# Hybrid block on one core: key layout with half the transposes, gate factors spread over the items, a fixed order at the start of the up-projection

## The chip, the cores and the metric

The kernel runs on one core of one Trainium2 chip. The metric is the time on the device in microseconds of one execution; the median of several runs counts. Before the change it is 2391.09 us, the median of three runs between 2388.72 and 2391.73. One more execution was taken with the profiler on, and all views of the trace are of that one.

## What is computed

One layer of a decoder block with 2048 tokens of width 1024, all in float32. Cut to what matters here:

```python
h = rmsnorm(x, attn_norm)
z = h @ w_in            # pool channels | q | k | v | gate_pool | gate_attn
a = pool_mixer(u_pool, w_pool, pool_scale)          # causal means, windows 2/4/8/16
q = partial_rope(rmsnorm(q, q_norm), positions) * scale
k = partial_rope(rmsnorm(k, k_norm), positions)     # 2 heads of 64 for 16 query heads
b = swa_sink_attention(q, k, v, sinks)              # window 128
x = x + (g_pool * a + g_attn * b) @ w_out
h = rmsnorm(x, ffn_norm)
up = causal_depthwise_conv(h @ w_up, conv_w, conv_b)   # 2 x 2816 wide
x = x + (silu(gate) * val) @ w_down
```

## The kernel before

The tokens are worked off in two chunks of 1024 (`c` = 0 and 1), channels in slabs of 128. Every float32 operand is split into a high and a low half in the type float32r: ScalarE (ACT) casts the high half, VectorE (DVE) subtracts it to get the low half, and a product is three matmuls, high x high, high x low, low x high. `parted` (L1066) does this for activations, `split` (L245) for ordinary weights, `halved` (L360) for the factors below.

**Keys.** For each block of 128 tokens `block_b` (L783) rotates two key heads of 64 and writes their halves into `kd`, each of them twice side by side, and `turn` (L794) transposes them on TensorE (PE): four 128 x 128 transposes, for two heads and two halves. Every transpose gives a tile with the same 64 key channels in the upper and in the lower 64 partitions. `kts[g]` holds for head g the high tile and the low tile over the chunk. In `scores` (L884) the stationary operand has the queries' high half in the upper 64 partitions and the low half in the lower 64, so that two matmuls per query head, one by each tile, give all four partial products. The last block's keys of chunk 0 go to DRAM (`carry`) for chunk 1.

**Fast products.** The gates, the output projection and the up-projection use a scheme of seven products in place of eight for blocks of 2 x 2 (Winograd's form of Strassen's). The weight side needs sums of blocks, called A11, A12, A22, S1 to S4; the activation side B11, B21, B22, T1 to T4. `Blocks` (L341) makes the weight side of one unit in four steps: `first` (A11, A12), `second` (A22 and two sums on DVE), then `third` (S3, S2) and `fourth` (two sums on DVE, then S1, S4); for the first two gate units the fourth comes before the third. Each step has a cast on ACT and a subtraction on DVE (L362 and L363 for a whole slab, L378 and L379 in the second step). The sums stand in L382, L383, L390 and L391. `store` (L353) writes finished factors of these units to DRAM (`kept`), where chunk 1 reads them again through `Kept`. `R` is the tag of the raw weights, with three buffers; a unit holds two of them until its steps are done.

**Attention items and fillers.** `mixer` (L1926) runs 32 items per chunk: four groups of four query heads, eight blocks of 128 tokens each. An item has the scores of one block, the probabilities of the item before and the values of the one before that; between them PE is filled with projections (`fillers`, L144). In the last group of chunk 0 the fillers are gate and pooling projections, and the items also make the factors of the first two gate units: unit 0 in items 1, 2 (two steps) and 3, unit 1 in items 5 and 7, each behind the item's softmax chain on DVE (`tc.issue_after(chain)`). `store` is called in items 1 to 4 just ahead of the step and writes out all that is made so far.

**Up-projection.** `up` (L1504) works off 22 units. A unit has the products `one` to `seven`: `one` A11 x B11, `two` A12 x B21, `three` S2 x T2, `four` S1 x T1, `five` S3 x T3, `six` S4 x B22, `seven` A22 x T4. `one`, `three`, `five` and `seven` add up in one PSUM bank `x`; between them the bank is read, by an ACT copy (`kept`, L1441) after `one` and `three` and by a DVE add (L1467) after `five`. `product` (L1248) issues the twelve matmuls of one product. The activation side is made at the start (the head): `right_t1` to `right_t4` and `right_b22`, each of a difference on DVE (T2: L1228, T3: L1235, T4: L1245) and a `parted`. The loop over the other units takes `seven` and `six` of one unit between the products of the next; `conv` (L1482) follows on ACT and DVE.

**Order.** No order is written out for the engines. A planner goes through the program, estimates durations and lays out each engine's stream: when an engine is free it takes the earliest instruction of the program that is ready by its estimate. `tc.issue_after(ins)` adds an edge: what the block issues on the engine of `ins` stands behind `ins` there. It is an order and no wait between engines. Each stream, and the queue of transfers that SP issues, is then worked off in order on the chip.

## Time and profile before

| | before |
|---|---|
| median of three runs | 2391.09 us (2388.72 to 2391.73) |
| profiled execution | 2387.73 us |
| its span, first to last instruction | 2386.0 us |
| mean granted clock of TensorE | 0.999 |
| transfers through HBM | 408.10 MB, mean 171 GB/s |

The span is what the page's shares refer to; the profiled execution's own time has 1.73 us around it. PE is a matmul, PEld the load of its stationary operand, SP the engine that issues most transfers. `L1252` is line 1252 of the kernel; where a helper such as `product` or `parted` issues an instruction, the line is the helper's, and the tile's name tells which part of the program it serves (`f`, `t`, `a`, `s` are PSUM banks; `U`, `M`, `Q`, `F`, `R` are tags of SBUF tiles). Rows of the timeline give the start, the length, the engine, line and operation with its tiles and shapes, how many neighbours are merged in the row, and in brackets the idle time of the engine before it with what ended it. Rows of the waits give the total idle time, how often, and the longest.

### The profile page before, as it was taken

What the parts mean: (1) busy time and instruction counts of PE and PEld (TensorE: products, weight loads), DVE (VectorE), ACT (ScalarE), POOL (GpSimd) and SP (SyncE); (2) the same over time, 40 slices, a digit from 0 to 9 for tenths busy, and PEclk for the clock granted to TensorE, in tenths of its full rate; (3) what the DMA queues carried; (4) which work ended last, traced back from release to release, by engine and by line L of the source; (5) the groups of instructions that cost most, each with busy time, mean ns of one, the idle gap of its engine ahead of it and who ended that gap; (6) DMA issues with size and microseconds to landing.
All of it is one profiled execution on the core that took longest, in us unless ns stands there. A gap on an engine that the chain in (4) does not pass through costs nothing.

```text
span 2386.0 us, 30215 instructions
## 1 busy us (share of the span) xinstructions
PE 2359.7 (99%) x11080; PEld 1960.6 (82%) x11080; DVE 1912.9 (80%) x2938; ACT 1177.0 (49%) x2148; POOL 190.8 (8%) x142
## 2 busy tenths in 40 slices
PE   9999999999999999999999999999999999999999
PEld 8888888888788888788888888888878888888887
DVE  8688888877977777899956867788798777779994
ACT  7555455464654555543622544454445545554441
POOL 1123121010000000000002232200000000000000
PEclk9999999999999999999999999999999999999999
DMA  9767778687222233644454776666733222228421
GB/s 343 246 199 239 224 213 292 222 336 259 79 93 90 88 107 108 215 164 157 141 194 143 230 217 194 199 205 231 239 125 103 80 80 80 80 74 288 141 71 53
DMA packets 165028, 408.10 MB, mean 171 GB/s; under 512 B 14096, under 2 KB 50448, under 8 KB 155152
## 3 DMA queue, kind: packets, MB, share of 16 engines
q1 hardware_dynamic: 151584, 373.48, 46.2%
q0 software_dynamic: 8256, 24.12, 4.2%
q10 hardware_dynamic: 5040, 8.58, 1.0%
q8 instruction: 87, 1.43, 0.2%
q14 instruction: 61, 0.50, 0.1%
HBM read 267.32 MB, written 138.81 MB: 170 GB/s over the span
## 4 chain that ended last, share of the span: by engine, by line
PE 52%; DVE 3%; DMA 1%; ACT 1%; issue 1%; POOL 0%; SPq 0%; DVEq 0%; ACTq 0%; POOLq 0%
PE f L1252 12%; PE f L266 8%; PE t L1252 7%; PE f L1907 4%; PE a L1907 4%; PE s L1907 4%; PE t L1907 4%; PE a L1252 3%; PE a L960 1%; PE a L266 1%; PE s L899 1%; PE t L932 0%; DMA U<-made_pg 0%; PE f L1296 0%; DVE U L1070 0%
## 5 line engine op out<-in xcount | busy, mean ns | idle before, releaser
L266 PE MATMUL f<-U,U 128*128 128x512 f32 (+1 forms) x2088 | 489.4, 388 | 4.6 <-DVE U L250 1.8
L1252 PE MATMUL f<-U,U 128*128 128x512 f32 x1872 | 445.2, 390 | 4.1 <-DVE U L1070 2.4
L266 PEld LDWEIGHTS f<-U,U 128*128 128x128 f32 x2088 | 380.2, 188 | 81.2 <-DVE U L250 3.3
L1252 PEld LDWEIGHTS f<-U,U 128*128 128x128 f32 x1872 | 350.8, 188 | 79.4 <-DVE U L1070 3.1
L1489 DVE SCALAR_TENSOR_TENSOR M<-F,vc,M 128x1024 f32<-128x1024 f32 x176 | 225.3, 1281 | 141.1 <-ACT M L1486 140.7
L1252 PE MATMUL t<-U,U 128*128 128x512 f32 x1332 | 314.3, 389 | 0.3 <-ACT Q L1441 0.3
L1252 PEld LDWEIGHTS t<-U,U 128*128 128x128 f32 x1332 | 249.7, 188 | 53.1 <-ACT Q L1441 0.9
L362 ACT CAST U<-R 128x1024 fp32r<-128x1024 f32 x147 | 153.8, 1053 | 86.6 <-DVE R L391 43.9
L1252 PE MATMUL a<-U,U 128*128 128x512 f32 x756 | 183.7, 390 | 0.7 <-ACT Q L1441 0.7
L363 DVE TENSOR_TENSOR U<-R,U 128x1024 fp32r<-128x1024 f32 x147 | 179.2, 1221 | 0.3 <-ACT U L362 0.3
L1252 PEld LDWEIGHTS a<-U,U 128*128 128x128 f32 x756 | 141.2, 188 | 30.2 <-ACT Q L1441 1.2
L1252 PE MATMUL f<-U,M 128*128 128x512 f32 x624 | 150.2, 389 | 0.3 <-DVE F L1467 0.3
L918 ACT ACTIVATE Q<-s,st,rq 128x128 f32<-128x128 f32 x256 | 114.0, 456 | 65.5 <-DVE st L915 62.1
L1252 PEld LDWEIGHTS f<-U,M 128*128 128x128 f32 x624 | 117.0, 188 | 25.0 <-DVE F L1467 0.7
L940 POOL TENSOR_SCALAR_AFFINE_SELECT M<-M 128x1024 fp32r<-128x1024 f32 x64 | 94.3, 1474 | 380.2 <-DVE st L920 206.8
L1475 ACT COPY F<-f 128x512 f32<-128x512 f32 x52 | 30.6, 588 | 185.1 <-PE f L1252 185.1
L1865 ACT CAST U<-U 128x1024 fp32r<-128x1024 f32 x76 | 79.0, 1050 | 84.5 <-PE s L1907 22.0
L1486 ACT ACTIVATE M<-F,vc 128x1024 f32<-128x1024 f32 x88 | 109.3, 1243 | 2.4 <-DVE F L1471 1.0
L1866 DVE TENSOR_TENSOR U<-U,U 128x1024 fp32r<-128x1024 f32 x76 | 91.9, 1218 | 2.6 <-ACT U L1865 2.4
L1865 ACT CAST F<-U 128x1024 fp32r<-128x1024 f32 x44 | 46.2, 1050 | 93.8 <-PE a L1907 62.5
L967 ACT COPY U<-a 128x512 f32<-128x512 f32 x64 | 37.5, 586 | 105.1 <-PE a L960 104.9
L1441 ACT COPY Q<-f 128x512 f32<-128x512 f32 x104 | 61.0, 586 | 56.2 <-PE f L1252 56.1
(319 smaller groups left out, 4086.0 us busy)
## 6 DMA issues: line engine op xcount, KB each, us to landing
R<-w_up SPq DMA_DIRECT2D x80, 512.0 KB, 3.7
actd<-M SPq DMA_DIRECT2D x44, 512.0 KB, 2.7
U<-w_down SPq DMA_DIRECT2D x88, 256.0 KB, 4.9
U<-actd SPq DMA_DIRECT2D x88, 256.0 KB, 5.0
qd<-U SPq DMA_DIRECT2D x64, 256.0 KB, 3.8
Q<-qd SPq DMA_DIRECT2D x64, 256.0 KB, 4.9
R<-w_out SPq DMA_DIRECT2D x30, 512.0 KB, 4.5
U<-kept_S SPq DMA_DIRECT2D x12, 1024.0 KB, 6.6
```

The lines of the kernel that those rows point to most:

```text
L266: nc.tensor.matmul(out, a, b, start=(i == 0), stop=(i == n - 1))
L362: A.copy(t[:, 0], raw)
L363: V.tensor_sub(t[:, 1], raw, t[:, 0].bitcast(F32))
L918: A.activation(pr[:, h, :], sc[:, h, 0:P], AF.Exp, bias=nm[:, h:h + 1], scale=it["rq"][:, h:h + 1], accum_out=rs[:, h:h + 1])
L940: G.affine_select(own.rearrange("p a h q -> p (a h) q"), pa.bitcast(F32).rearrange("p a h q -> p (a h) q"), pattern=[[0, 8], [1, P]], base ...
L1252: nc.tensor.matmul(bank, a[:, x, k, :], b[k // 2][:, y, k % 2, :], start=(first and i == 0), stop=(i == 11), skip_group_check=True)
L1441: Up.last = A.copy(t, bank).ins
L1486: A.activation(y, u[:, 2:], AF.Identity, bias=cw[:, 3, m:m + 1], scale=cw[:, 2, m:m + 1])
L1489: V.scalar_tensor_tensor(y, u[:, j:j + T], cw[:, j, m:m + 1], y, op0=ALU.mult, op1=ALU.add)
L1865: A.copy(hi, src)
L1866: V.tensor_sub(lo, src, hi.bitcast(F32))
L1907: nc.tensor.matmul(into[m], u[:, 0, c_], v[:, 1], start=(first and j == 0), stop=(k == n - 1 and j == 2), skip_group_check=True)
```

## The change

Three parts of the kernel are changed.

1. Keys: `kd` holds for each head the high half in columns 0 to 63 and the low half in columns 64 to 127, so two transposes per block do; a transposed tile has the high half above and the low half below. `kts[0]` gets it by one DVE copy, `kts[1]` with the two halves exchanged by two ACT copies of 64 partitions. The scores use `kts[0]` and `kts[1]` where they used the high and the low tile; the sum of the two matmuls is the same.
2. Gate factors: unit 0's steps go to items 1, 2 and 3, and one to item 4 ahead of that item's fillers, behind the last weight split's cast on ACT. `store` writes in items 2 to 5 only what was made at least one item before.
3. Head of the up-projection: from `u0.four` to the end of the unit 3 round every product stands behind the product before it on PE. The first T3 difference stands behind the second T2 difference, the second T3 difference behind the second T2 tile's low half. T4 and the first later step of unit 2 stand behind T3's last low half on DVE. `u1.five` moves ahead of `u0.seven`.

```diff
-        def store(self, f, dma=load):
+        def store(self, f, only=None, dma=load):
...
-                if names not in done:
+                if names not in done and (only is None or names in only):
...
-            kd = kds[n] = qp.tile([P, 2, 2, P], F32R, "Q")
-            for d in range(2):
-                A.copy(kd[:, :, 0, d * HD:(d + 1) * HD], kn)
-                V.tensor_sub(kd[:, :, 1, d * HD:(d + 1) * HD], kn,
-                             kd[:, :, 0, d * HD:(d + 1) * HD].bitcast(F32))
+            kd = kds[n] = qp.tile([P, 2, P], F32R, "Q")
+            A.copy(kd[:, :, 0:HD], kn)
+            V.tensor_sub(kd[:, :, HD:P], kn, kd[:, :, 0:HD].bitcast(F32))
...
-            pt = ps.tile([P, 2, 2, P], F32R, "t")
+            pt = ps.tile([P, 2, P], F32R, "t")
             for g in range(2):
-                for a in range(2):
-                    nc.tensor.transpose(pt[:, g, a, :], kd[:, g, a, :], identr)
-            for g in range(2):
-                V.tensor_copy(kts[g][:, :, c_], pt[:, g].bitcast(F32))
+                nc.tensor.transpose(pt[:, g], kd[:, g], identr)
+            V.tensor_copy(kts[0][:, :, c_], pt.bitcast(F32))
+            for i in range(2):
+                A.copy(kts[1][64 * i:64 * i + 64, :, c_],
+                       pt[64 - 64 * i:128 - 64 * i].bitcast(F32))
...
-    def right_t3(xg, b):
+    def right_t3(xg, b, after=()):
         for j in range(2):
             q12, q22 = half(xg[j], 1), half(xg[j + 2], 1)
-            V.tensor_sub(q12, q22, q12)
+            with tc.issue_after(after[j]) if after else nullcontext():
+                V.tensor_sub(q12, q22, q12)
             b.setdefault("T3", []).append(parted(q12))
...
+        ordered = False
+
         def mul(self, bank, x, y, first=False):
-            product(bank, self.w.w[x], self.b[y], first)
+            with tc.issue_after(product.last) if Up.ordered else nullcontext():
+                product(bank, self.w.w[x], self.b[y], first)
...
         t2s = right_t2(xg, b, pb)
+        Up.ordered = True
         u0.four()
         u0.w.fetch("A22")
-        right_t3(xg, b)
+        right_t3(xg, b, (right_t2.sub, right_t2.low))
+        third = parted.low
...
         u0.five()
-        right_t4(xg, b, t2s)
-        weights(2, 1)
+        with tc.issue_after(third):
+            right_t4(xg, b, t2s)
+            weights(2, 1)
         u0.six()
         yg = u0.conv(0, u0.ug)
+        u1.five()
         u0.seven()
...
-        u1.five()
         for f in range(2, FT + 1):
+            Up.ordered = f < 4
...
             for g in range(2):
-                load(carry[g, :, 0:2], kts[g][:, :, T - P:T].bitcast(F32))
+                for a in range(2):
+                    load(carry[g, :, a], kts[a][:, g, T - P:T].bitcast(F32))
...
+            if c == 0 and group == 3 and n == 4:
+                with tc.issue_after(split_weights.last[0]):
+                    units[0].w.step()
...
                     if n == 0:
+                        older = []
                         stream.fetch(stream.used + 2)
-                    for f, steps in enumerate(({1: 1, 2: 2, 3: 1, 4: 0}, {5: 1, 7: 1})):
+                    for f, steps in enumerate(({1: 1, 2: 1, 3: 1, 4: 0, 5: 0}, {5: 1, 7: 1})):
                         if n in steps:
+                            w = units[f].w
                             if f == 0:
-                                units[f].w.store(units[f].f)
+                                w.store(units[f].f, older)
+                                older = list(w.tiles)
                             with tc.issue_after(chain):
-                                units[f].w.step(steps[n])
+                                w.step(steps[n])
```

More of the change, by code (lines that the diff above doesn't have):

```diff
@@ L886, in scores @@
         b = c * NB + n
-        kt = it["kts"][g]
+        kt = [t[:, g] for t in it["kts"]]
         if n == 0 and q4 == 3:
@@ L898, in scores @@
                 if n > 0:
-                    nc.tensor.matmul(sc[:, h, :], st, kt[:, a, (n - 1) * P:(n + 1) * P], **fl)
+                    nc.tensor.matmul(sc[:, h, :], st, kt[a][:, (n - 1) * P:(n + 1) * P], **fl)
                 else:
-                    nc.tensor.matmul(sc[:, h, P:256], st, kt[:, a, 0:P], **fl)
+                    nc.tensor.matmul(sc[:, h, P:256], st, kt[a][:, 0:P], **fl)
             if n == 0 and b > 0:
@@ L1069, in parted @@
         A.copy(t[:, 0], src)
-        V.tensor_sub(t[:, 1], src, t[:, 0].bitcast(F32))
+        parted.low = V.tensor_sub(t[:, 1], src, t[:, 0].bitcast(F32)).ins
         return t
@@ L1138, in out_proj @@
                     elif n * KT + m == at + 5:
-                        made.store(f, G.dma_start)
+                        made.store(f, dma=G.dma_start)
                 if n == 0 and m == 4:
@@ L1227, in right_t2 @@
             t2s.append(mp.tile([P, 2, 512], F32, "M"))
-            V.tensor_sub(t2s[j], half(xg[j + 2], 1), half(xg[j], 0))
+            right_t2.sub = V.tensor_sub(t2s[j], half(xg[j + 2], 1), half(xg[j], 0)).ins
             b.setdefault("T2", []).append(parted(t2s[j]))
+            right_t2.low = parted.low
         return t2s
-    def right_t3(xg, b):
+    def right_t3(xg, b, after=()):
         for j in range(2):
             q12, q22 = half(xg[j], 1), half(xg[j + 2], 1)
-            V.tensor_sub(q12, q22, q12)
+            with tc.issue_after(after[j]) if after else nullcontext():
+                V.tensor_sub(q12, q22, q12)
             b.setdefault("T3", []).append(parted(q12))
@@ L1251, in product @@
             for x, y in ((0, 0), (0, 1), (1, 0)):
-                nc.tensor.matmul(bank, a[:, x, k, :], b[k // 2][:, y, k % 2, :],
-                                 start=(first and i == 0), stop=(i == 11),
-                                 skip_group_check=True)
+                product.last = nc.tensor.matmul(bank, a[:, x, k, :], b[k // 2][:, y, k % 2, :],
+                                                start=(first and i == 0), stop=(i == 11),
+                                                skip_group_check=True).ins
                 i += 1
```

## The prediction, made before the changed kernel was run

> **What bounds the kernel now.** I read the page's first part (busy time of each engine) first, then the waits of TensorE, then the busy time by stage, and only then the order of single instructions around the longest waits.
>
> ```profile
> span 2386.0 us, 30215 instructions
> PE 2359.7 (99%) x11080; PEld 1960.6 (82%) x11080; DVE 1912.9 (80%) x2938; ACT 1177.0 (49%) x2148; POOL 190.8 (8%) x142
> ...
> PE f L1252 <- DVE U L1070: 2.4, 2, 1.3
> ...
> PE f L1252 <- ACT Q L1441: 1.4, 2, 0.7
> ...
> 575.00:645.00 70.00, 68.28 (x309) 55.88 (x308) 59.53 (x63) 35.77 (x52) 1.04 (x1) 1.00 0.40 146
> 1220.00:1305.00 85.00, 85.00 (x494) 74.54 (x493) 50.34 (x174) 25.05 (x69) 16.43 (x10) 1.00 0.43 139
> 1750.00:1815.00 65.00, 62.72 (x276) 50.96 (x275) 60.23 (x67) 34.43 (x44) 1.01 (x1) 1.00 0.24 81
> ```
>
> TensorE (PE) is the bound: it is busy 2359.7 of 2386.0 us, so 26.3 us of idle time is all that better order can win; anything else has to come from fewer PE instructions. The two wait rows (total, times, longest) are products of the up-projection (L1252) that wait for split operands (L1070) or for a bank to be copied out (L1441); both lie in code that the diff touches. The window rows give the length of the stage, then busy PE, weight loads, DVE, ACT and POOL. The two heads of the up-projection (575 to 645 and 1750 to 1815) have PE idle 1.7 and 2.3 us with DVE busy 85% and 93%: DVE sets the pace there. In the second chunk's keys (1220 to 1305) PE is never idle, so each transpose removed there comes straight off the end.
>
> **Keys by half the transpositions.**
>
> ```profile
> 1263.57 0.46 PE L799 MATMUL t<-identr,Q 128*128 128x128 f32 x4
> 1263.86 0.94 PE L266 MATMUL a<-U,U 128*128 128x256 f32 x6
> ...
> L799 PE MATMUL t<-identr,Q 128*128 128x128 f32 x64 | 7.2, 241 | 0.0
> L801 DVE CAST U<-t x32: 406/414/425, 42.3 to 1301.3; 128x256 fp32r<-128x256 f32 x32
> L790 ACT CAST Q<-Q x32: 293/298/308, 34.4 to 1279.9; 128x128 fp32r<-128x128 f32 x32
> L791 DVE TENSOR_TENSOR Q<-Q,Q x32: 274/285/295, 35.5 to 1280.2; 128x128 fp32r<-128x128 f32 x32
> L708 ACT COPY F<-f x16: 351/373/377, 12.1 to 72.0; 128x256 f32<-128x256 f32 x16
> ```
>
> A block of keys takes four transposes now and two after; 16 blocks make 32 fewer. Starts tell the price, since neighbours overlap: four begin at 1263.57 and the next matmul at 1263.86, so 0.29 us for four, 0.072 each, and 32 x 0.072 = 2.3 us. Their busy time shared out (7.2/64 = 0.112) would make it 3.6 us. I take 2.5, near the starts, because the busy figure counts overlap with the neighbours. [...]
>
> DVE loses one L791 and one L801 per block, 0.285 + 0.414 = 0.70 us. ACT loses one L790 and gains two copies of 64 partitions x 256 from PSUM; the nearest row is L708 (128x256 from PSUM, 373 ns), so ACT has 2 x 0.373 - 0.298 = 0.45 us more per block. In the second chunk both are hidden, since PE has no idle time there. In the first chunk's keys both engines feed PE closely, so the effect is bounded by one block's relief, -0.7, and one block's added ACT time, +0.45; I take -0.2. The two extra carry transfers happen once and lie on SP ahead of loads of weights and queries; at some 0.33 us of issue each (the SP rows below) they cost nothing as long as those loads land early, and 0.7 us at most.
>
> **Gate factors, one step per item.**
>
> ```profile
> 352.41 1.20 PE L266 MATMUL f<-U,U 128*128 128x512 f32 x4 [1.78 <-ACT U L249]
> ...
> 354.43 0.74 PE L266 MATMUL f<-U,U 128*128 128x512 f32 x2 [0.51 <-DVE U L250]
> ...
> 350.08 0.68 DVE L391 TENSOR_TENSOR R<-R,R 128x512 f32<-128x512 f32 x1
> ...
> 350.80 1.04 ACT L362 CAST U<-R 128x1024 fp32r<-128x1024 f32 x1
> 351.75 0.61 ACT L249 CAST U<-R 128x512 fp32r<-128x512 f32 x1
> ```
>
> The number in brackets is the idle time before a group and what ended it. Here PE stops 1.78 us for the high half of a pooling weight (L249), then 0.51 us for the low half (L250). On ACT that cast stands right behind L362, the cast of the gate unit's fourth step, which could begin only when DVE had finished L391 at 350.76. This is item 2 of the last group, the one with two steps; with one step the fourth moves to item 3, and L249 no longer stands behind it. PE's matmuls start 0.23 us apart but are drawn 0.39 long, so a stop costs about 0.16 more than its bracket: 1.78 + 0.51 + 2 x 0.16 = 2.6 us. I take 2.3, leaving 0.3 for what is late next; the bounds are 2.6 and nothing (the stop moves to item 3 or 4). The third step moves to item 4 and is put behind the last split's cast on ACT, so it cannot stand in front of that one. Each store to DRAM goes an item later, which takes its wait for L363 or L379 off SP; the copies are read in the second chunk only. One raw half of the unit is held an item longer, so the next unit's second raw half loads later; that is used only at item 7 and stays hidden.
>
> **The up-projection's head.**
>
> ```profile
> 600.46 1.21 DVE L1228 TENSOR_TENSOR M<-U,U 128x1024 f32<-128x1024 f32 x1
> 601.60 2.35 DVE L1235 TENSOR_TENSOR U<-U,U 128x1024 f32<-128x1024 f32 x2
> 603.87 1.21 DVE L1070 TENSOR_TENSOR U<-M,U 128x1024 fp32r<-128x1024 f32 x1
> ...
> 602.35 1.75 PE L1252 MATMUL f<-U,U 128*128 128x512 f32 x7
> 605.14 1.42 PE L1252 MATMUL f<-U,U 128*128 128x512 f32 x5 [1.04 <-DVE U L1070]
> 607.23 2.14 PE L1252 MATMUL f<-U,U 128*128 128x512 f32 x8 [0.67 <-ACT Q L1441]
> ...
> 1769.44 1.52 PE L1252 MATMUL f<-U,U 128*128 128x512 f32 x6
> 1771.23 0.50 PE L1252 MATMUL f<-U,U 128*128 128x512 f32 x1 [0.26 <-ACT U L1069]
> 1773.07 1.43 PE L1252 MATMUL f<-U,U 128*128 128x512 f32 x5 [1.34 <-DVE U L1070]
> 1775.18 1.20 PE L1252 MATMUL f<-U,U 128*128 128x512 f32 x4 [0.68 <-ACT Q L1441]
> ```
>
> In the first chunk PE stops in the middle of u0's third product, until the low half of the second T2 tile (L1070 at 603.87) is there. Both T3 differences (L1235) stand before it. With the new order only the first of them does; the low half then runs at 602.8 and ends about 604.0, and PE wants it at 603.9: the stop of 1.04 shrinks to about 0.2. The next stop, 0.67, is u0's fifth product, which follows its third at once and has to wait until ACT has copied the shared bank out (L1441). In strict order u1's third product stands between them and covers that copy. So 1.04 + 0.67 + 2 x 0.16 = 2.0 us go and 0.2 comes back. In the second chunk the same three stops make 0.26 + 1.34 + 0.68 + 3 x 0.16 = 2.8 us.
>
> What is late next: a unit's seventh product writes on the bank that the DVE add behind its fifth (L1467) must have read. Strict order puts u1's seventh right behind u0's, so one product stands between u1's fifth and seventh.
>
> ```profile
> 618.28 2.88 PE L1252 MATMUL f<-U,U 128*128 128x512 f32 x12
> 621.00 2.88 PE L1252 MATMUL t<-U,U 128*128 128x512 f32 x12
> ...
> 625.01 0.69 DVE L1467 TENSOR_TENSOR F<-f,Q 128x512 f32<-128x512 f32 x1
> ...
> 1786.21 2.88 PE L1252 MATMUL f<-U,U 128*128 128x512 f32 x12
> ...
> 1790.88 0.68 DVE L1467 TENSOR_TENSOR F<-f,Q 128x512 f32<-128x512 f32 x1
> ...
> 613.10 0.32 SPq L243 DMA_DIRECT2D M<-kept_A  x1
> 620.45 0.33 SPq L243 DMA_DIRECT2D R<-w_up  x1
> ...
> 1786.18 0.33 SPq L243 DMA_DIRECT2D R<-w_up  x1
> 1786.56 0.42 SPq L243 DMA_DIRECT2D M<-kept_A  x1
> ...
> DMA to landing us min/median/max: 3.1/6.1/9.4
> ```
>
> A product is 621.00 - 618.28 = 2.72 us. From the end of u1's fifth to the end of its add it took 621.16 to 625.70, 4.5 us, and in the second chunk 1789.09 to 1791.56, 2.5 us. Against one product of cover that is a stop of 1.8 and of nothing. The fifth now stands earlier in the program, so its add goes ahead of the value convolution; I take 0.4 in each chunk. The later sevenths have two products of cover, 5.4 us, and cost nothing. Moving T4 behind T3's last low half changes no count: from 600.46 twelve DVE operations at 1.14 us end near 614, and T4 is wanted at 616 (602.35 plus five products).
>
> First head: -2.0 + 0.2 + 0.4 = -1.4. Second: -2.8 + 0.4 = -2.4. **The sum** is -2.5 - 0.2 - 2.3 - 1.4 - 2.4 = -8.8 us. The profiled execution took 2387.73 us, of which 2386.0 are its span; it would become 2378.9. It lies 3.4 us below the median of the three runs, 2391.09, against which the result will stand, so I forecast 2391.09 - 8.8 = **2382.3**.
>
> **The rivals.** *Second operand late* (20%): u1's seventh also needs A22 (M<-kept_A), which comes by SP. In the second chunk that load stood behind a load of raw weights which had to wait until 1786.18, and was issued at 1786.56; with 3.1 us (the shortest landing of this tensor's transfers, last row above) to their median of 6.1 it lands between 1789.7 and 1792.7. Strict order wants it at 1769.44 + 6 x 2.72 = 1785.8. If the queue keeps that order, PE stops some 5.4 us: -8.8 - 0.4 + 5.4 = -3.8, 2387.3. For it: SP works in order. Against it: in the first chunk the same load went ahead, at 613.10, as soon as its slot was free.
>
> *DVE is the bound in the heads* (18%): with 85 and 93% busy, what PE gains in front it waits for a few products later, at the sevenths or at the next unit's factors. Both heads then give nothing: -2.5 - 0.2 - 2.3 = -5.0, 2386.1. It is also what happens if the new order of sums does not do what it says.
>
> *Slower* (6%): the A22 load is late in both chunks. In the first it would go behind R<-w_up, issued 620.8 and landing 623.9 to 626.9, against u1's seventh at 602.35 + 6 x 2.72 = 618.7: 6.7 us. Then -2.5 - 0.2 - 2.3 - 4.8 + 0.2 + 6.7 + 5.4 = +2.5, 2393.6. It decides from the point where the two stops together pass 9.6 us. A stop that long may also lower the clock, as it fell in this stretch of the second chunk's out-projection:
>
> ```profile
> 1725.50:1729.00 3.50, 3.50 (x11) 2.69 (x9) 0.43 (x1) 0.00 (x0) 0.07 (x1) 0.53 1.07 324
> ```
>
> The granted clock was 0.53 for 3.5 us, worth 1.75 us; twice that gives 2397.1. The 1.78 us stop at 352.41 drew no such row. [...]
>
> **How the numbers follow.** The forecast has 53%, its own range 2379 to 2386; 3% is left for other changes of order, since the planner lays out every engine's stream anew when some durations and edges change. The best ends of all terms (-3.6 - 0.7 - 2.6 - 2.0 - 2.8) make -11.7, 2379.4; the three runs before spread by 3 us, so the range begins at 2378.5. It ends at 2390.0, above the two rivals that stay below the old time. About 0.2%, 4.8 us, is what a measurement of this kernel can tell from no change. Faster by more: nearly all of the forecast and some of the DVE rival, 57%. Within: the late operand, the rest of the DVE rival and the edge of the forecast, 36%. Slower: 7%.
>
> **What would show it.** Right: L799 with 32 transposes and some 2.5 us less PE time; no wait on L249 near 352; no L1070 wait of a microsecond and no L1441 wait inside either head; PE idle in the two head windows under 1 us each. Wrong: a bracket on the first matmul of u1's seventh (f<-U,M) that names L1467 or a DMA from kept_A; a new wait on L249 or L250 an item later; a new low clock in the heads.

## The result and the profile after

The changed kernel is slower. Its median is 2406.01 us (six runs, 2401.07 to 2408.88) against 2389.95 us for the kernel before, run beside it; the ratio is 1.0066, with a 95% interval of 1.0056 to 1.0076. The forecast was 2382.3 us, and its range ended at 2390.0. The profiled execution took 2403.85 us, 2402.1 of them its span.

The first part of the page and the busy time in the two stretches of the heads, for the changed kernel (length of the stretch, then busy PE, weight loads, DVE, ACT and POOL, then the granted clock):

```profile
span 2402.1 us, 30149 instructions
PE 2360.1 (98%) x11048; PEld 1961.7 (82%) x11048; DVE 1907.4 (79%) x2906; ACT 1187.8 (49%) x2164; POOL 189.9 (8%) x142
...
575.00:645.00 70.00, 62.81 (x277) 50.85 (x276) 57.60 (x61) 35.27 (x49) 1.04 (x1) 0.98 0.38 137
...
1750.00:1815.00 65.00, 56.13 (x240) 45.04 (x240) 57.19 (x66) 31.73 (x41) 1.01 (x1) 0.95 0.30 106
```

PE has 32 instructions fewer, as meant, but is busy as long as before, since matmuls took longer where the clock fell (12 of them 4.34 us behind the longest stop of the first head, 2.88 otherwise; last section). Its idle time rose from 26.3 to 2402.1 - 2360.1 = 42.0 us. Both heads of the up-projection lost: PE is idle there 7.2 and 8.9 us, where it was 1.7 and 2.3, and DVE is busy for less time than before in both, not for more. The next view says on what PE waits (total, times, longest):

```profile
PE f L1253 <- DMA M<-kept_A: 9.2, 2, 4.7
PE s L898 <- ACT Q L917: 6.1, 2, 5.5
...
PE f L1253 <- DVE F L1471: 3.1, 3, 1.4
PE f L1253 <- ACT Q L1445: 2.3, 2, 1.2
```

The products are L1253 now, formerly L1252. New are four waits: for A22 (`kept_A`), the long one of the scores (L898) for the exponentials of the gates' items (L917), the one for the add behind a fifth product (L1471, formerly L1467), and the one for the copy of a bank (L1445, formerly L1441) at another product than before. The waits on the low half of T2 (formerly L1070) are gone.

Where each stage begins is read from the first TensorE instruction of the stage. The differences of the stage lengths to the kernel before, in us, for every kernel of this study (the runs are described below; "out + up" is the output projection with the up-projection, c0 and c1 are the first and the second chunk, which the expectations call chunk 1 and chunk 2). Each row is one profiled execution, and one fall of the clock put some 1.5 to 2.8 us on the stage that it hit, by the estimates of the last section:

| kernel | keys c0 | items c0 | gates c0 | out + up c0 | keys c1 | items, gates c1 | out + up c1 | span |
|---|---|---|---|---|---|---|---|---|
| before (length) | 123.35 | 257.02 | 104.54 | 517.82 | 83.14 | 363.71 | 505.87 | 2386.0 |
| after | -0.60 | -3.01 | +6.85 | +6.35 | -1.33 | -0.34 | +8.35 | +16.1 |
| e1_keys | -0.22 | +0.15 | +1.14 | +0.38 | -1.33 | -0.35 | -1.31 | -1.7 |
| e2_gates | -0.03 | -2.92 | 0.00 | +0.22 | -0.01 | +0.06 | +2.52 | -0.2 |
| e3_head | -0.04 | +0.99 | 0.00 | +6.83 | -0.01 | +0.03 | +7.59 | +15.4 |
| e4_a22 | +0.47 | -3.07 | +6.49 | +9.28 | -1.33 | -0.47 | +4.39 | +15.7 |
| e6_upto3 | -0.57 | -3.03 | +6.82 | -1.51 | -1.33 | -0.41 | -3.08 | -3.3 |
| e7_weights | -0.71 | -3.06 | +7.21 | +9.38 | -1.36 | -0.23 | +6.94 | +18.0 |
| e9_keysgates | -0.52 | -3.07 | +7.95 | +0.91 | -1.33 | -0.58 | -1.18 | +2.0 |
| e10_slot | -0.56 | -3.05 | +5.85 | +0.29 | -1.33 | -0.65 | -2.65 | -2.2 |
| e11_hand | -0.53 | -3.07 | +7.65 | +2.36 | -1.33 | -0.36 | +0.01 | +4.6 |
| e12_upto5 | -0.71 | -3.00 | +5.97 | +4.62 | -1.33 | -0.67 | +2.05 | +6.8 |
| e13_nokeys | -0.26 | -2.89 | +0.83 | -0.83 | -0.01 | -0.39 | -3.54 | -7.1 |
| e14_nogates | -0.74 | +0.17 | +0.15 | -0.73 | -1.33 | -0.62 | -2.84 | -6.1 |

Three stages lost: 6.85 + 6.35 + 8.35 = 21.55 us. The others gave 5.3 back. That this is close to what the prediction gave them (5.0) is luck: the keys gave 1.9 in place of 2.7, the items 3.0 in place of 2.3.

**The first head.** The timeline of the changed kernel in the first chunk, PE first, then DVE, ACT and SP (start, length, engine, line, operation, and in brackets the idle time before it and what ended it):

```profile
617.37 3.06 PE L1253 MATMUL f<-U,U 128*128 128x512 f32 x12 [1.15 <-ACT Q L1445]
621.81 3.04 PE L1253 MATMUL f<-U,M 128*128 128x512 f32 x12 [1.38 <-DVE F L1471]
629.50 4.34 PE L1253 MATMUL f<-U,M 128*128 128x512 f32 x12 [4.65 <-DMA M<-kept_A]
...
619.94 1.22 DVE L363 TENSOR_TENSOR U<-R,U 128x1024 fp32r<-128x1024 f32 x1
621.07 0.68 DVE L1471 TENSOR_TENSOR F<-f,Q 128x512 f32<-128x512 f32 x1
621.67 1.22 DVE L363 TENSOR_TENSOR U<-R,U 128x1024 fp32r<-128x1024 f32 x1
...
623.41 1.22 DVE L363 TENSOR_TENSOR U<-R,U 128x1024 fp32r<-128x1024 f32 x1
624.87 0.69 DVE L382 TENSOR_TENSOR R<-R,R 128x512 f32<-128x512 f32 x1 [0.24 <-DMA R<-w_up]
625.47 2.60 DVE L1493 SCALAR_TENSOR_TENSOR M<-F,vc,M 128x1024 f32<-128x1024 f32 x2
628.18 0.69 DVE L1471 TENSOR_TENSOR F<-f,Q 128x512 f32<-128x512 f32 x1
...
615.79 1.05 ACT L1068 CAST U<-U 128x1024 fp32r<-128x1024 f32 x1 [3.49 <-DVE U L1246]
616.74 0.58 ACT L1445 COPY Q<-f 128x512 f32<-128x512 f32 x1
...
621.18 2.07 SPq L243 DMA_DIRECT2D R<-w_up  x2
623.35 0.38 SPq L243 DMA_DIRECT2D M<-kept_A  x1
```

The three PE rows are u1's fifth, u0's seventh and u1's seventh product. Each starts late, and each for another engine. u1's fifth waits for the copy of u1's third from the bank: on ACT that copy stands behind a cast of T4 that waited 3.49 us for DVE. u0's seventh waits for u0's fifth add: on DVE it stands behind unit 2's rows, L363 being the last of them. u1's seventh waits for two things that come at nearly the same time: u1's fifth add, which ended at 628.87 because three L363, two other adds (L1471 and, not shown, L1475), L382 and two passes of the gate half's convolution (L1493) went ahead of it, and A22, which SP issued at 623.35 behind two raw loads and which took 6.0 us to land, 629.4. After that last stop 12 matmuls take 4.34 us where they take 2.88 otherwise. The second chunk's head shows the same three stops: 1.19, 1.39 and 4.59 us.

**The gates.** In the first chunk the same view of ACT and PE at item 7, and the tile `tad` (the attention result in DRAM) in 370 to 392 us:

```profile
379.50 2.19 ACT L1670 ACTIVATE U<-U,vc 128x1024 f32<-128x1024 f32 x2 [3.80 <-DMA U<-xT]
387.39 0.59 ACT L966 COPY U<-a 128x512 f32<-128x512 f32 x1 [5.70 <-DMA tad<-U]
...
389.80 2.08 PE L898 MATMUL s<-U,Q 128*128 128x256 f32 x8 [5.49 <-ACT Q L917]
...
L971 POOL DMA_DIRECT2D tad<-U x1: 1022/1022/1022, 376.0 to 376.0; - x1
...
DMA to landing us min/median/max: 4.4/7.8/11.2
```

L966 copies attention values into a new `U` tile. That tile got the buffer of the tile before it, which POOL's adding transfer (issued 376.0, landed 11.2 us later, at 387.2) was still reading. The copy waits 5.70 us for it, the exponentials stand behind the copy on ACT, and PE waits for the exponentials. The semaphores in the trace of the kernel before show that there a load of `xT` into a `U` tile was the next to wait for that transfer, so the new attention tile had another buffer.

### The profile page after: what moved, and what is told of

It reads as the page before. It is cut to its first block, busy times and chain, and to the rows that moved or that the text cites. A ratio compares the mean times of both kernels' runs of the same rounds, so it can differ in the third digit from the quotient of the medians.

```text
span 2402.1 us, 30149 instructions
## 1 busy us (share of the span) xinstructions
PE 2360.1 (98%) x11048; PEld 1961.7 (82%) x11048; DVE 1907.4 (79%) x2906; ACT 1187.8 (49%) x2164; POOL 189.9 (8%) x142
## 3 DMA queue, kind: packets, MB, share of 16 engines
q8 instruction: 87, 1.43, 0.2%
## 4 chain that ended last, share of the span: by engine, by line
PE 86%; DVE 7%; DMA 3%; ACT 2%; issue 1%; POOL 0%; SPq 0%; DVEq 0%; ACTq 0%; POOLq 0%
PE f L1253 22%; PE f L266 16%; PE t L1253 12%; PE a L1253 6%; PE f L1915 4%; PE a L1915 4%; PE s L1915 4%; PE t L1915 4%; PE f L1098 4%; PE a L959 2%; PE s L898 2%; PE a L266 2%; DVE U L1069 1%; PE t L931 1%; PE s L1297 1%
## 5 line engine op out<-in xcount | busy, mean ns | idle before, releaser
L1253 PE MATMUL f<-U,U 128*128 128x512 f32 x1872 | 446.5, 391 | 2.3 <-ACT Q L1445 2.3
L1253 PEld LDWEIGHTS f<-U,U 128*128 128x128 f32 x1872 | 352.7, 189 | 77.4 <-ACT Q L1445 3.4
L1493 DVE SCALAR_TENSOR_TENSOR M<-F,vc,M 128x1024 f32<-128x1024 f32 x176 | 225.4, 1282 | 149.4 <-ACT M L1490 148.9
L1253 PE MATMUL t<-U,U 128*128 128x512 f32 x1332 | 314.5, 389 | 0.3 <-ACT Q L1445 0.2
L1253 PEld LDWEIGHTS t<-U,U 128*128 128x128 f32 x1332 | 249.7, 188 | 53.3 <-ACT Q L1445 0.8
L362 ACT CAST U<-R 128x1024 fp32r<-128x1024 f32 x147 | 154.0, 1053 | 84.6 <-DVE R L383 41.9
L1253 PE MATMUL a<-U,U 128*128 128x512 f32 x756 | 183.5, 390 | 0.7 <-ACT Q L1445 0.7
L363 DVE TENSOR_TENSOR U<-R,U 128x1024 fp32r<-128x1024 f32 x147 | 179.3, 1222 | 2.1 <-ACT U L362 2.0
L1253 PEld LDWEIGHTS a<-U,U 128*128 128x128 f32 x756 | 141.2, 188 | 30.2 <-ACT Q L1445 1.2
L1253 PE MATMUL f<-U,M 128*128 128x512 f32 x624 | 153.4, 395 | 12.4 <-DMA M<-kept_A 9.2
L1253 PEld LDWEIGHTS f<-U,M 128*128 128x128 f32 x624 | 118.8, 191 | 39.2 <-DVE F L1471 14.4
L917 ACT ACTIVATE Q<-s,st,rq 128x128 f32<-128x128 f32 x256 | 114.0, 456 | 54.6 <-DVE st L914 54.6
L966 ACT COPY U<-a 128x512 f32<-128x512 f32 x64 | 37.5, 586 | 106.8 <-PE a L959 100.8
L1098 PE MATMUL f<-U,U 128*128 128x512 f32 x384 | 87.9, 390 | 0.0
```

Of the source, the lines that this page charges most:

```text
L362: A.copy(t[:, 0], raw)
L363: V.tensor_sub(t[:, 1], raw, t[:, 0].bitcast(F32))
L917: A.activation(pr[:, h, :], sc[:, h, 0:P], AF.Exp, bias=nm[:, h:h + 1], scale=it["rq"][:, h:h + 1], accum_out=rs[:, h:h + 1])
L1098: nc.tensor.matmul(po, w[:, a, k, :], ms[k // 2][n][:, b, k % 2, :], start=(first and i == 0), stop=(last and i + 1 == len(order)))
L1253: product.last = nc.tensor.matmul(bank, a[:, x, k, :], b[k // 2][:, y, k % 2, :], start=(first and i == 0), stop=(i == 11), skip_group_che ...
L1493: V.scalar_tensor_tensor(y, u[:, j:j + T], cw[:, j, m:m + 1], y, op0=ALU.mult, op1=ALU.add)
```

## The experiments

All times are medians beside runs of the kernel before on the same chip (2389.2 to 2389.7 us in the four sets).

**One part at a time.** Three kernels: before with the keys' edits alone, with the gate factors' edits alone, with the head's edits alone.

> The kernel before with the key part of the change alone. Theory (the keys are a small gain and not the cause): 32 fewer transposes save about 2 us, 2388 against 2390, and the stops of the gate stage and of the two heads stand as before (1.0 and 1.3 us for L1070 in the heads). Rival (the keys part makes the planner lay out the gate stage anew, and the 5.5 us stop at 389 comes from it): the stop is there, and the time is 2393 or more.

Measured 2388.31 us, ratio 0.9994 (0.9984 to 1.0003), which is not clear of no change. The second chunk's keys became 1.33 us shorter for 16 transposes, 0.083 us each; the first chunk's only 0.22, and there PE waits 2.0 us for high halves of split weights from ACT (L249), which it did not before, and 1.4 for their low halves from DVE (L250), before 2.5.

> The kernel before with the gate-factor part alone. Theory: the stop of 1.8 us for L249 near 352 goes (-2.5 to -3 us in the items), but the ACT copy of the last attention tile waits for the transfer of the tile before it (about 5.5 us, and a us of lower clock after it): together +4 us, 2394. Rival (that stop belongs to the three parts together): only the gain is seen, 2387.

Measured 2386.25 us, ratio 0.9984 (0.9975 to 0.9993). The items became 2.92 us shorter and the gates' stage is unchanged: the stop at item 7 doesn't come from this part alone.

> The kernel before with the up-projection's head alone. Theory (strict order makes u1's seventh product wait for its A22, which stands behind two loads of raw weights on SP): a stop of about 4.7 us at u1's seventh in both chunks and about 1.7 us of lower clock behind it, the up-projection 6 to 8 us longer in each chunk, 2404. Rival (in the changed kernel the load is late because of the other two parts): the stages are shorter than before by 1 to 2 us each, 2387.

Measured 2402.53 us, ratio 1.0048 (1.0031 to 1.0066). The head's part alone makes the loss in both heads, with the same waits and lengths (u1's seventh waits 4.40 and 4.32 us for A22).

**The A22 load.** The whole change, with u1's load of A22 put right behind u0's, so that it no longer stands behind the raw weights on SP.

```diff
         u0.four()
-        u0.w.fetch("A22")
+        for u in (u0, u1):
+            u.w.fetch("A22")
         right_t3(xg, b, (right_t2.sub, right_t2.low))
...
-        u1.w.fetch("A22")
```

> The changed kernel with one line moved: u1's A22 is asked for right behind u0's, ahead of T3, so that its load stands ahead of the raw weights on SP. Theory (queue position is the cause): the stop at u1's seventh and the lower clock behind it go in both chunks, 2 x (4.7 + 1.7) = 13 us, 2393. Rival (DVE is the bound there, the stop only moves to the adds or to the next unit's factors): less than half of it comes back, 2400 or more.

Measured 2400.41 us, ratio 1.0045 (1.003 to 1.006). The chain of causes is seen in two rows of this kernel, PE's seventh product of u1 and the add that it waits for:

```profile
631.17 5.06 PE L1253 MATMUL f<-U,M 128*128 128x512 f32 x11 [4.02 <-DVE F L1471]
...
630.42 0.69 DVE L1471 TENSOR_TENSOR F<-f,Q 128x512 f32<-128x512 f32 x1
```

The load is early now and the stop is still 4.02 us, put down to the add. So A22 was one of two late inputs, and the profile of the changed kernel named only the later one. The median is 5.6 us below the changed kernel's, of four runs against six in another set; the two profiled spans differ by 0.4 us. The second head's stage is 4.0 us shorter and the first's 2.9 longer, and the records of the clock go with that: this execution has one short fall fewer in the second and a longer one in the first, where u1's seventh takes 5.06 us for 11 matmuls (4.34 for 12 in the changed kernel); the mean over the span is 0.996 in both. That the load is worth more than the 0.6 us of the stop is not shown.

**The keys with the gate factors.** Before with both parts, without the head's.

> Before, with the keys' part and the gate factors' part, without the head's part. Theory: the stop of 5.5 us at item 7 of the gates comes from these two parts together (the new attention tile gets a buffer of which POOL's adding transfer still reads), so the gates' stage takes 110 to 111 us as in the changed kernel, and the time is before's 2389.7 less 1.4 (keys) less 3.5 (gates) plus 6.5, about 2391 us. Rival: it takes the head's part too, the gates' stage stays at 104.5 us, and the parts add up: about 2385 us.

Measured 2389.76 us, ratio 1.0002 (0.9993 to 1.0012), and the gates' stage is 7.95 us longer. The stop at item 7 comes with these two parts together and needs nothing of the head; neither of them has it alone.

**The strict order shortened.** The whole change, but the products are ordered by hand only through u1's third.

```diff
         u1.three()
+        Up.ordered = False
...
         for f in range(2, FT + 1):
-            Up.ordered = f < 4
```

> The changed kernel whole, but the strict order of the up-projection's products ends after u1's third product: from u0's fifth product on they stand in the order that the planner gives them, all edges on T3, T4 and B22 and the place of u1's fifth product being kept. Theory: the strict order over the fifth to seventh products is what makes the planner put the eight VectorE rows of unit 2's operands ahead of u0's fifth add and the convolution's passes ahead of u1's fifth add, so that u1's seventh product stops for it and the clock falls behind the stop. Without it both stops of 4.6 us at u1's seventh product go, with their half-clock matmuls (about 1.7 us each) and the 1.4 us stops on u0's fifth add: 7 to 8 us less in chunk 1's head and as much in chunk 2's, about 2391 us, the stop of 5.5 us at item 7 of the gates remaining. Rival: the edges on T3 and T4, which queue VectorE's sums late, set it: the stops stay and the time is 2404 to 2406 us.

Measured 2386.28 us, ratio 0.9991 (0.9981 to 1.0): 19.7 us less than the changed kernel, hardly clear of the kernel before. PE and DVE of this kernel in the first head:

```profile
609.27 3.04 PE L1253 MATMUL f<-U,U 128*128 128x512 f32 x12 [1.26 <-ACT Q L1445]
...
617.81 2.88 PE L1253 MATMUL f<-U,U 128*128 128x512 f32 x12
620.53 2.88 PE L1253 MATMUL f<-U,M 128*128 128x512 f32 x12
623.25 2.88 PE L1253 MATMUL t<-U,U 128*128 128x512 f32 x12
625.97 2.65 PE L1253 MATMUL a<-U,U 128*128 128x512 f32 x11
...
628.81 3.00 PE L1253 MATMUL f<-U,M 128*128 128x512 f32 x12
...
613.31 0.68 DVE L1471 TENSOR_TENSOR F<-f,Q 128x512 f32<-128x512 f32 x1
...
625.10 0.69 DVE L1471 TENSOR_TENSOR F<-f,Q 128x512 f32<-128x512 f32 x1
```

u1's fifth product begins at 617.81 and its seventh at 628.81; u0's seventh, u2's third and u1's sixth lie between, and none of them stops. One stop is left in this head, of 1.26 us, at u0's fifth (609.27), which waits for the copy of u0's third. u1's fifth add begins 4.4 us after the product's end (625.10 against 620.69; it was 628.18 against 620.43, 7.75 us, in the changed kernel), and u0's fifth add goes ahead of unit 2's rows, at 613.31. The edges on T3 and T4 are all still there, so the strict order beyond u1's third makes the loss of the heads; the gates' stage keeps its own (+6.82).

**Unit 2's weights outside the edge.** The whole change, with `weights(2, 1)` behind T4 moved out of the block with the edge.

> The changed kernel whole, but the step of unit 2's weights that stands behind T4 is outside the edge on T3's last low half; T4 itself stays behind it. Theory (the strict order sets the ranks): u0's fifth add comes hardly earlier and u1's fifth add still lies behind the convolution, so u1's seventh product stops for 4 to 5 us in both chunks and the time is 2403 to 2407 us. Rival: unit 2's rows, pushed by that edge in front of the adds, are what makes them late: the stops on the adds go to under 1 us, what is left is A22's transfer, and the time is 2394 to 2400 us.

Measured 2404.74 us, ratio 1.0065 (1.0048 to 1.0081): u1's seventh still waits 3.35 us in the first chunk and 5.26 in the second, both times for L1471. That edge isn't the cause.

**Strict, but in another order.** The whole change with its strict order; only u1's seventh product goes behind u2's third and u1's sixth.

```diff
         for f in range(2, FT + 1):
...
-            old.seven()
-            old.value()
-            weights(f + 1, 1)
+            if f > 2:
+                old.seven()
+                old.value()
+                weights(f + 1, 1)
             u.three()
...
             old.six()
+            if f == 2:
+                old.seven()
+                old.value()
+                weights(f + 1, 1)
```

> The changed kernel whole, its strict order too, but u1's seventh product stands behind u2's third and u1's sixth instead of ahead of them. Theory (the wrong place in the strict order: u1's seventh has one product, 2.6 us, between itself and u1's fifth, and needs the add of it): with three products between, 7.7 us, add and A22 are there in time, both stops of 4.6 us go with the half-clock matmuls behind them, and the time falls by 10 to 13 us to 2393 to 2396 us; the stops of 1.2 and 1.4 us ahead of them and the one in the gates stay. Rival (strictness itself: any order fixed by hand makes VectorE's rows late by as much again): the stop moves to another product, and the time stays above 2400 us.

Measured 2393.21 us, ratio 1.0019 (1.001 to 1.0028), 12.8 us less than the changed kernel, inside what the theory gave. PE and DVE of this kernel:

```profile
618.19 3.02 PE L1253 MATMUL f<-U,U 128*128 128x512 f32 x12 [1.15 <-ACT Q L1445]
622.63 3.01 PE L1253 MATMUL f<-U,M 128*128 128x512 f32 x12 [1.43 <-DVE F L1471]
625.49 2.88 PE L1253 MATMUL t<-U,U 128*128 128x512 f32 x12
628.21 2.88 PE L1253 MATMUL a<-U,U 128*128 128x512 f32 x12
631.00 3.00 PE L1253 MATMUL f<-U,M 128*128 128x512 f32 x12
...
629.21 0.69 DVE L1471 TENSOR_TENSOR F<-f,Q 128x512 f32<-128x512 f32 x1
```

The add is as late as in the changed kernel (it begins at 629.21, 8.0 us after the end of u1's fifth at 621.21), but three products now cover it and the 4.65 us stop is gone. Against the shortened order 2393.21 - 2386.28 = 6.9 us remain. Here each head has stops of about 1.2, 1.4 and 1.4 us (the last for a fifth's add at u2's seventh), 4.0 in all, where the shortened order has the one of 1.26; the rest is not accounted for, but the clock of this execution fell for longer in the gates.

**Another buffer in the gates.** The kernel with the shortened order, and the second gate unit's first step one item later, which changes the order in which `U` buffers are taken.

```diff
-                    for f, steps in enumerate(({1: 1, 2: 1, 3: 1, 4: 0, 5: 0}, {5: 1, 7: 1})):
+                    for f, steps in enumerate(({1: 1, 2: 1, 3: 1, 4: 0, 5: 0}, {6: 1, 7: 1})):
```

> The kernel of the run with the strict order only up to u1's third product, with one more edit: in the gates of chunk 1 the step of the second unit's factors stands at item 6 instead of item 5. Theory (which buffer the new attention tile gets decides the stop): the tile now gets a buffer that POOL's adding transfer doesn't read, ACT's copy doesn't wait, the stop at 390 us goes and the gates' stage falls from 111.4 to about 104.5 us: 2386.3 less 6 to 7, about 2379.5 us. Rival (POOL's transfers are late in any case, or the step one item later makes the second gate's operands late): the stage stays above 109 us and the time at 2385 us or above.

Measured 2385.77 us, ratio 0.9981 (0.9972 to 0.999), within half a microsecond of the kernel that it starts from. The gates' stage is still 110.4 us. ACT, PE, and the tile `tad` of this kernel:

```profile
378.48 0.59 ACT L966 COPY U<-a 128x512 f32<-128x512 f32 x1 [3.74 <-issue]
387.71 1.04 ACT L362 CAST U<-R 128x1024 fp32r<-128x1024 f32 x1 [1.96 <-issue]
...
388.81 1.22 PE L1253 MATMUL f<-U,U 128*128 128x512 f32 x2 [2.51 <-ACT U L362]
...
L362 ACTq EVENT_SEMAPHORE  x1: 5561/5561/5561, 382.1 to 382.1; - x1
...
L971 POOL DMA_DIRECT2D tad<-U x1: 1019/1019/1019, 376.1 to 376.1; - x1
...
DMA to landing us min/median/max: 4.5/8.0/11.5
```

The first half of the theory holds: with another buffer L966 no longer waits for the transfer. But the buffer went to the next taker. The cast of the second unit's factor (L362) begins at 387.71, just when the transfer landed (376.1 + 11.5 = 387.6), and PE waits 2.51 us for that cast. Its bracket names no releaser, but in front of it ACT's queue stands in a semaphore wait of 5.56 us from 382.1 on, and one of the two semaphores of that wait is the transfer's. The wait had moved, and the clock fell behind it: the stage and the time are those of the rival.

**The strict order one product longer.** The kernel of the last run, with the strict order through u0's fifth.

> The kernel of the run with the step at item 6, with the strict order kept one product longer, through u0's fifth: u1's third then lies between u0's third and fifth. Theory: the stop of 1.4 us at u0's fifth product (it waits for ACT's kept copy of the third) goes in both chunks and no other comes: 2.5 us less than that run, about 2377 us. Rival: as with the whole strict order, what PE doesn't wait for there it waits for at the next products, and the time is that run's within 1 us or above it.

Measured 2394.05 us, ratio 1.0016 (1.0006 to 1.0026), 8.3 us above it: the theory missed. Two of PE's longest waits in this kernel, and a stretch behind them:

```profile
PE t L1253 <- ACT U L1068: 4.4, 2, 2.2
...
PE t L1253 <- DVE U L1069: 2.7, 2, 1.4
...
612.70:616.40 3.70, 3.65 (x9) 2.88 (x10) 3.70 (x4) 0.00 (x0) 0.00 (x0) 0.50 0.02 4
```

The wait for u0's bank copy is gone as expected, and PE waits at u0's sixth product (bank `t`) 2.2 us for the high and 1.4 us for the low half of a split operand, in each chunk, and the clock is halved behind these stops (last row, from the first chunk: 0.50). The first matmuls of the sixth products, which stood behind u0's fifth, stand behind u0's third now, before their operand is made. The edge on one product changed where the planner put others.

**Without the conflict.** Before with two parts each: the gate factors with the shortened head, and the keys with the shortened head.

> Before, with the gate factors' part and the head's part, the strict order ending after u1's third product; the keys as before. Theory: without the keys' part the last attention tile of chunk 1 gets a buffer that POOL's transfer has left, so there is no stop at 390 us and the gates' stage takes 104.5 us; the items keep the 3 us of the gate factors, the heads the 2.0 and 1.3 us of the run that ends the strict order there: 2389.6 less 3.5 less 3.3, about 2383 us, faster than before and than the changed kernel. Rival: some other stop takes the place of the one in the gates, or the clock falls at the row statistics of chunk 2 as in the run of the gate factors alone (2.8 us): 2385.5 to 2387 us.

Measured 2384.33 us (2380.59 to 2388.23), ratio 0.9979 (0.997 to 0.9988). No stop at item 7 (gates +0.83), items -2.89, out + up -0.83 and -3.54.

> Before, with the keys' part and the head's part, the strict order ending after u1's third product; the gate factors as before. Theory: the keys give 1.4 us as in their own run, the heads 3.3 us, and there is no stop at 390 us: about 2385 us. Rival: the keys' part changes the buffers here too and brings a stop in the gates of 1 to 6 us: 2386 to 2391 us.

Measured 2384.55 us, ratio 0.9981 (0.9973 to 0.999), gates +0.15. Both beat the kernel before and the changed one; they cannot be told apart. The semaphores of the traces tell who waits next for POOL's transfer, and so who got its buffer. With the keys' and the gate factors' part it is the attention copy (L966), or L362 in the two kernels with the step at item 6. With the gate factors' part alone (e2_gates, e13_nokeys) it is a cast at 390.5 and 390.9 us, which comes after the landing at 388.0 and 388.4. Without that part (before, e1_keys, e3_head, e14_nogates) it is a load of `xT` from SP.

## Why the prediction was wrong

**What bounds the kernel** was right: PE, with DVE close behind in the heads. Idle time of PE is nearly all that was lost, 15.7 of 16.1 us of span.

**Keys.** The term was -2.5 - 0.2. Measured in the second chunk: -1.33. Measured in the first: -0.22 alone, -0.60 in the whole change. The price per transpose (0.083 us, taken 0.078) was right; mis-sized was the count. Only the second chunk's 16 stand where PE is never idle. In the first chunk's keys PE waits for DVE and ACT, as the prediction itself says, and the 16 transposes there gave little or nothing: e13_nokeys, which has the old keys, shows -0.26 in this stage.

**Gate factors.** The term was -2.3, between -2.6 and nothing; the items gave between -2.89 and -3.07 in every kernel with this part, more than its bound; where the rest comes from is not shown. What failed is that the gates' stage stood at nothing in the sum: the prediction follows the moved steps through the queues and through the raw weights' `R` buffers ("stays hidden") only. A step also takes a `U` buffer, and moving it changes which buffer later tiles get. Together with the keys' part the new attention tile got one that a transfer of 11.2 us was still reading: +6.85 us, nothing of which was in the sum or in a rival. That the two parts together lead to that buffer, and either alone does not, is shown by e1_keys, e2_gates, e9_keysgates, e13_nokeys and e14_nogates; why the planner chooses it then is not shown.

**The heads.** The stops that were to go (L1070, then L1441 at u0's fifth) went. The step that failed is the price of what is late next: "its add goes ahead of the value convolution; I take 0.4 in each chunk". The add does go ahead of the value convolution; but the gate half's convolution and unit 2's rows stand ahead of the add. From the product's end to the add's end it took 8.4 us (620.43 to 628.87), where the prediction has 4.5 and 2.5 from the kernel before. u0's seventh, with the stop ahead of it, covers 4.4 of them (it ends at 624.85), which leaves 4.0; A22 landed 0.5 us later still, and the stop was 4.65, in the second chunk 4.59. I took DVE's order before as the order after, although the planner lays out each engine by its estimates, and e6_upto3 against the changed kernel shows that the strict order on PE by itself changed DVE's order. Against e9_keysgates, which has the rest of the change, the head's part cost 6.35 - 0.91 = 5.4 us in the first chunk and 8.35 + 1.18 = 9.5 in the second, where -1.4 and -2.4 were forecast. With the strict order ended after u1's third it gave -2.4 and -1.9, near the forecast.

**"Moving T4 behind T3's last low half changes no count"** held for DVE: from the second T2 difference to the end of the second T4 difference it takes 12.7 us, formerly 12.6. It left out ACT, where the T4 cast waits for that difference and holds up the copy of u1's third bank (1.15 us).

**The rivals.** The late second operand was right in mechanism for both chunks: SP's order held A22 back behind the raw loads, and PE's bracket named it. But e4_a22 shows that without it the add takes its place within about 0.6 us (4.02 against 4.65), so alone it decided little. The rival that DVE becomes the bound was right about the place (the sevenths) and wrong about the size: it assumed that PE can wait for no more than it had gained. The slower rival had the right place, and with the clock its 2397.1 came nearest; it lacked the stop in the gates (6.85) and the two smaller stops per head.

## What to carry to other kernels

An order by hand on one engine fixes more than that engine: a planner that estimates when results appear can reorder the others. Before fixing it, list for every product the one that frees its bank and count the products between, then ask how much the freeing engine has queued. A saved instruction was worth its time here only in the stage where its engine never idles: 16 transposes gave 1.33 us in the second chunk's keys, where PE is busy all the time, and 0.22 us in the first's, where it waits. A step moved between pooled buffers must be followed to every later taker of those buffers. When a wait has two late inputs, ask for both: here the profile named the later one (A22, a stop of 4.65 us), and with that one alone removed the other took its place (the add, 4.02 us).

## What the hardware showed

The granted clock fell behind the stops. Three stretches of the changed kernel, from u1's seventh in the first chunk, from the row statistics of the second and from item 7 of the gates on; then one of the kernel with another buffer in the gates, one of the kernel in another strict order, and one of e3_head (the granted clock is the number ahead of the last two):

```profile
629.40:633.20 3.80, 3.70 (x10) 3.00 (x11) 2.81 (x3) 3.33 (x5) 0.00 (x0) 0.61 0.00 0
...
1759.00:1762.60 3.60, 3.60 (x11) 2.74 (x10) 1.56 (x2) 0.00 (x0) 0.60 (x1) 0.56 0.56 221
389.70:393.40 3.70, 3.60 (x13) 3.22 (x14) 3.43 (x7) 3.18 (x6) 1.09 (x1) 0.50 0.27 48
```

```profile
388.80:392.40 3.60, 3.59 (x11) 2.95 (x12) 3.34 (x4) 2.64 (x3) 0.00 (x0) 0.55 0.46 182
```

```profile
622.60:626.20 3.60, 3.57 (x16) 2.96 (x17) 3.15 (x4) 2.54 (x4) 0.00 (x0) 1.00 0.55 163
```

```profile
353.10:356.60 3.50, 3.35 (x9) 2.15 (x8) 3.50 (x10) 3.17 (x11) 0.15 (x1) 0.51 0.52 168
```

Stops of 4.65, 5.49 and also 2.51 us were followed by a granted clock of 0.61, 0.50 and 0.55; one of 1.43 us (the fifth row) by 1.00. Length alone didn't decide. The stop of 1.79 us at 352 in e3_head was followed by a granted clock of 0.51 (the last row), the same stop of the kernel before (1.78 us) by 1.00 in the same stretch. In the run of the gate factors alone the stops of 0.26 and 1.34 us in the second chunk's head were followed by a granted clock of 0.50 from 1772 to 1776 us, and the same two stops of the kernel before by 1.00 from 1768 to 1776. From 1768 to 1780 us, in steps of 4 us, the run of the gate factors alone has a granted clock of 0.81, 0.50 and 0.84 with PE busy for 2.39, 3.33 and 4.00 us; by these the fall is worth some 2.8 us, an estimate, near the +2.52 of that run in the table, in a stage where it changes nothing.

In the clock record of the changed kernel the granted clock is 0.50 from 386.63 to 393.46 us, from 628.98 to 632.39, from 1758.79 to 1762.20 and from 1803.16 to 1806.58, one fall behind the last matmul aside: 6.83 us once and 3.41 us three times. The four begin 71, 331 and 13 times 3.413 us apart. The kernel before has one such fall, 3.41 us from 1725.35 on. Part of such a stretch can lie in the stop itself: of the first, 3.17 us lie ahead of the end of the stop at 389.80, of the second, 0.52 us ahead of 629.50. The loss of the three rows of the changed kernel, estimated from their length and granted clock, is (1 - 0.61) x 3.8 = 1.5 us to (1 - 0.50) x 3.7 = 1.9 us, for the two stops a third again of the stop itself. In the first head of e12_upto5 the granted clock is 0.63 from 610.6 to 613.7 us, 0.50 from 612.7 to 616.4 and 0.75 from 616.4 to 620, together a fall of about 6.8 us; with 5.5 us of PE's work in it, it loses 2.7 by the same estimate.

At the row statistics (L655, which sums squares for the norm) the clock fell with 0.83 and 0.88 us of idle time. The first two of eight rows of the changed kernel just ahead of that stretch (six more of two matmuls each follow without a stop, the last at 1757.95):

```profile
1755.36 0.35 PE L655 MATMUL a<-one,F 128*128 128x1 f32 x2 [0.83 <-DVE F L1338]
1756.59 0.38 PE L655 MATMUL a<-one,M 128*128 128x1 f32 x2 [0.88 <-ACT M L1334]
```

These sixteen matmuls of 128x1, 2.9 us in all with stops of 0.83 us ahead of them and 0.88 us among them, were followed by a granted clock of 0.50, as in the kernel before with one stop of 0.38 us. In e1_keys the same sixteen with a stop of 0.37 us were not (mean over the span 1.000), nor in e6_upto3 without a stop (1.00 from 1690 to 1745 us). Why the clock fell in the one and not in the other is not shown.
